# A two-layer decoder trunk on one core: the fourth token form laid with the others, and the first weight unit of each group laid apart

## The chip, the core and the metric

The kernel runs on one core of one Trainium2 chip. The metric is the device time of one execution in microseconds. The kernel before takes 1856.49 us, the median of three runs (1855.77 to 1856.5).

## What is computed

The reference is a decoder trunk of two layers over 512 tokens of width 1024, all in float32. Each layer is a feed-forward, a token mixer with memory heads beside it, and a second feed-forward, each followed by a layer norm of the scaled residual:

```python
x = layer_norm(DN_ALPHA * x + 0.5 * swiglu(x, ffn_w_gu[layer, 0], ffn_w_down[layer, 0]), ...)
o_tok, q_mem = mla_mix(...) if layer < N_A_LAYERS else nsa_mix(...)
o_mem = memory_attention(q_mem, mem, w_mem_kv[layer])
x = layer_norm(DN_ALPHA * x + jnp.concatenate([o_tok, o_mem], -1) @ w_out[layer], ...)
x = layer_norm(DN_ALPHA * x + 0.5 * swiglu(x, ffn_w_gu[layer, 1], ffn_w_down[layer, 1]), ...)
```

The first layer's mixer is latent attention, the second's a sparse attention of three branches. The four feed-forwards, `swiglu(x, w_gu, w_down) = (silu(x @ w_g) * (x @ w_u)) @ w_down` with an inner width of 2816, are most of the work, and the change is in them.

## The kernel before

**Split numbers.** TensorE multiplies float32 in a rounded form (`F32R`), so every operand is split in a high part and the rest: `split` (line 194) makes the high part by a cast on ScalarE (L199) and the low part by a subtraction on VectorE (L200). A product is three matmuls: high by high, high by low, low by high. Weights come in units of 128 partitions x 1024 floats, 512 KB each. `prep` (line 154) loads the next unit of a fixed order into `wraw` by a DMA from the SP queue, takes a pair of tiles `whi` and `wlo` for it, and splits it. The pair comes from `wring` (three pairs) or, inside the feed-forward scopes, from `W.extra` (four pairs more) in turn. `_unit_order` (line 53) writes that order out, and `unit(name, idx, look)` hands out the next pair after preparing units up to `look` further on.

**The feed-forward.** `ffn(l, f, ...)` (line 457) works on 22 column blocks (each 128 columns of w_g and the same 128 of w_u), which `GROUPS` cuts into five groups. A block of kind "s" is done plainly: two units, each multiplied with all of x by `feature_major` (L363, L365, L368: 48 matmuls of 256 columns a unit, 24 for each half of the tokens). A block of kind "d" is done by `seven` (line 482): the two 1024 x 128 matrices and the two halves of the tokens are a 2 x 2 product in blocks, and it is computed with seven products instead of eight, from sums and differences of the weights (`combined`, line 131, units g0 to g3) and of the tokens. One of the seven products is a `quarter` (line 370), 12 matmuls of 256 columns:

```python
for k in range(4):
    nc.tensor.matmul(ps, lhsT=hi[:, ks], rhs=xh[:, k], ...)   # L376
    nc.tensor.matmul(ps, lhsT=hi[:, ks], rhs=xl[:, k], ...)   # L377
for k in range(4):
    nc.tensor.matmul(ps, lhsT=lo[:, ks], rhs=xh[:, k], ...)   # L380
```

The order in a block is: unit g0 with the inputs themselves twice (`quarters(0, 0)`, `quarters(1, 0)`); unit g1 with form 4 and then form 1; unit g2 with forms 2 and 3; unit g3 with the inputs once (`quarters(1, 1)`). The four forms are sums and differences of the token blocks, made once for a feed-forward by `token_forms` (line 388) and kept split, each in two tiles `t1h`, `t1l` to `t4h`, `t4l` of the pool `F.fm`, called `t` in the profile. In the matmul the weights are the stationary operand and the tokens the moving one.

After the blocks of a group come its down projections (`by_units`, or `token_major` for the last group): there the activations `hhi`, `hlo` are stationary and the weight units `whi`, `wlo` move, 512 columns a matmul (L411 to L416, in the last group also L351 to L353). Then the next group begins with a g0 unit. In the first group of ffn(0,0), ffn(0,1) and ffn(1,1) (`halves` is true) three plain blocks come first: their six units are gone through for the first 256 tokens and then for the second 256. In ffn(1,0) two plain blocks come first, unit by unit.

**Where tiles lie.** A pool's tiles lie one behind the other in the order of their first use, pools on the left grow up from the bottom of SBUF, those opened by `right_pool` down from the top. Tiles called "place" or "offset" are never written: they fix the order, or shift what follows. `open_f` (line 262) lays out `F.fm` in that way, with a shift of 80 floats (320 bytes) ahead of form 4. A pool with `reuse_waits="tile"` makes a new tile wait for those older tiles that lay where it lies.

**What sets the order.** Within one engine's queue the framework issues by readiness and program order in its own model of time; only a few DMAs are pinned. TensorE's matmuls stand in the order that the program names.

Of the kernel before, what the change touches and what calls it, by code (L numbers as in the profile page):

```python
# [9 lines left out]
F32 = mybir.dt.float32  # L10
F32R = mybir.dt.float32r
# [6 lines left out]
P = 128  # L18
T = 512
# [32 lines left out]

def _unit_order():

    order = []

    def ffn(l, f, s):
        for m0, items in _groups(l, f):
            m = m0
            for it in items:  # L60
                if it == "d":
                    order.extend((f"g{i}", (l, f, m), 1024, s) for i in range(4))
                else:
                    order.extend(("gu", (l, f, m, g), 1024, s) for g in range(2))
                m += 1
            for i in range(m0, m):
                order.append(("dn", (l, f, i), 1024, s))

    ffn(0, 0, 0)
    for l in range(2):  # L70
        for i in range(4):
            order.append(("wm", (l, i), 1024, 0))
    for i in range(4):
        order.append(("wc", (i,), 832, 0))
    for i in range(2):
        order.append(("wqm", (i,), 1024, 0))
    order.append(("wuv", (), 768, None))
    order.append(("wuk", (), 768, None))
    for i in range(3):
        order.append(("wuq", (i,), 1024, None))  # L80
    for k in MIXORDER:
        order.append(("wo", (0, k), 1024, 1))
    ffn(0, 1, 1)
    for i in range(4):
        order.append(("wkf", (i,), 1024, 1))
    for i in range(2):
        order.append(("wvv", (i,), 1024, 1))
    for j in range(2):
        for i in range(4):
            order.append(("w1", (j, i), 1024, 1))  # L90
    for j in range(2):
        order.append(("w2", (j,), 256, 1))
    ffn(1, 0, 1)
    for i in range(3):
        order.append(("wgq", (i,), 876, 1))
    for i in range(6):
        order.append(("wq", (i,), 1024, 1))
    for k in MIXORDER:
        order.append(("wo", (1, k), 1024, 2))
    ffn(1, 1, 2)  # L100
    return order


@with_exitstack
def tile_trunk(ctx: ExitStack, tc, a: dict, out):
    nc = tc.nc
    order = _unit_order()

    const = ctx.enter_context(tc.tile_pool(name="const", bufs=1))
    wraw = ctx.enter_context(tc.tile_pool(name="wraw", bufs=NRAW))  # L110
# [7 lines left out]
    class W:  # L118
        pos = 0
        done = 0  # L120
        scope = None
        extra = None
        count = 0
        early = 0
        ready = {}
# [28 lines left out]
    def prep():  # L154
        name, idx, n, scope = order[W.done]
        if name in ("g0", "g1", "g2", "g3"):
            raw = combined(name, idx)
            n = 512 if name == "g3" else n
        else:
            src = a[name]  # L160
            for i in idx:
                src = src[i]
            raw = load(src, n)
        pool, tag = wring, "r"
        if scope is not None and W.scope is not None:
            W.count += 1
            if W.count % (NRING + NEXTRA) in EXTRA:
                pool, tag = W.extra, "x"
        hi = pool.tile([P, 1024], F32R, tag=tag + "h", name="whi")
        lo = pool.tile([P, 1024], F32R, tag=tag + "l", name="wlo")  # L170
        eng = nc.vector
        for c in ((slice(0, n),) if W.done else (slice(0, 512), slice(512, 1024))):
            split(hi[:, c], lo[:, c], raw[:, c], eng=eng)
        W.ready[W.done] = (hi, lo)
        W.done += 1
# [87 lines left out]
    def open_f(scope):  # L263
        F.st = ExitStack()
        W.extra = F.st.enter_context(tc.tile_pool(name=f"wx{scope}", bufs=NEXTRA, reuse_waits="tile"))
        F.xp = F.st.enter_context(tc.tile_pool(name=f"xp{scope}", bufs=1, reuse_waits="tile"))
        F.xp.tile([P, 112], F32, name="offset")
        F.sm = F.st.enter_context(tc.tile_pool(name=f"sm{scope}", bufs=2, reuse_waits="tile"))
        F.x = [F.xp.tile([P, D], F32, name=f"x{t}") for t in range(NT)]
        F.bk = 0  # L270
        W.scope = scope
        W.count = 0
        F.fst = ExitStack()
        F.fm = F.fst.enter_context(tc.tile_pool(name=f"fm{scope}", bufs=1, reuse_waits="tile"))
        for i in (1, 2, 3, 0, 4):
            for e in "hl":
                if i:
                    F.fm.tile([P, 4, 256], F32, tag=f"t{i}{e}", name="place")
            if not i:
                F.fm.tile([P, 80], F32, name="offset")  # L280

    def close_f():
        F.st.close()
# [4 lines left out]
    def right_pool(name, bufs=1):  # L288
        st = ExitStack()
        pool = st.enter_context(tc.tile_pool(name=name, bufs=bufs, side="right", reuse_waits="tile"))  # L290
        return st, pool
# [164 lines left out]

    def ffn(l, f, i, halves, spill=None, final=False, mid=None, hook=None):
        hst, hp = right_pool(f"h{l}{f}")
        if hook is None:
            load_gb(l, i)  # L460
        groups = _groups(l, f)
        for gi, (m0, items) in enumerate(groups):
            n = len(items)
            hhi = hp.tile([P, 5, T], F32R, tag="hhi", name="hhi")
            hlo = hp.tile([P, 5, T], F32R, tag="hlo", name="hlo")

            def fbank():
                F.bk += 1
# [1044 lines left out]
```

## Time and profile before

| | |
|---|---|
| median of 3 runs | 1856.49 us |
| the profiled execution | 1857.48 us |
| its span, first to last instruction | 1855.6 us |
| mean granted clock | 0.997 |
| TensorE busy | 1833.6 us (99%) |
| VectorE / ScalarE busy | 1463.0 us (79%) / 869.6 us (47%) |
| 256-column matmuls of `quarter`, L376, L377, L380 | 2156 on each line |

A matmul's duration in the profile includes the way through the array, so matmuls that follow one another overlap: what one costs in a stream is the distance from its start to the next start. In the timeline, matmuls of one kind that follow each other are drawn together (x4, x8). PEld is the loading of the stationary operand for the next matmul, which runs beside the present one.

### The profile page before, as it was taken

What the parts mean: (1) busy time and instruction counts of PE and PEld (TensorE: products, weight loads), DVE (VectorE), ACT (ScalarE), POOL (GpSimd) and SP (SyncE); (2) the same over time, 40 slices, a digit from 0 to 9 for tenths busy, and PEclk for the clock granted to TensorE, in tenths of its full rate; (3) what the DMA queues carried; (4) which work ended last, traced back from release to release, by engine and by line L of the source; (5) the groups of instructions that cost most, each with busy time, mean ns of one, the idle gap of its engine ahead of it and who ended that gap; (6) DMA issues with size and microseconds to landing.
All of it is one profiled execution on the core that took longest, in us unless ns stands there. A gap on an engine that the chain in (4) does not pass through costs nothing.

```text
span 1855.6 us, 31915 instructions
## 1 busy us (share of the span) xinstructions
PE 1833.6 (99%) x12776; PEld 1652.6 (89%) x12776; DVE 1463.0 (79%) x2362; ACT 869.6 (47%) x1435; POOL 162.6 (9%) x185
## 2 busy tenths in 40 slices
PE   9999999999999999999999999999999999999998
PEld 8899899896789899899999998998956789999997
DVE  7798788758668789788897987987567478887887
ACT  6344345456645345334653433444466444434432
POOL 0000000025500000000100000001255200000000
PEclk9999999999999999999999999999999999999999
DMA  6333334530234234234433323334321224323322
GB/s 241 114 114 103 125 103 146 177 114 24 69 114 145 75 102 134 80 103 148 130 120 113 126 84 110 114 121 158 110 46 29 113 75 131 114 80 114 118 81 75
DMA packets 59700, 203.85 MB, mean 110 GB/s; under 512 B 6944, under 2 KB 7216, under 8 KB 59552
## 3 DMA queue, kind: packets, MB, share of 16 engines
q1 hardware_dynamic: 56848, 194.18, 32.5%
q0 software_dynamic: 2416, 7.11, 1.2%
q8 instruction: 101, 1.65, 0.4%
q10 hardware_dynamic: 288, 0.52, 0.1%
q14 instruction: 47, 0.39, 0.1%
HBM read 188.16 MB, written 7.34 MB: 105 GB/s over the span
## 4 chain that ended last, share of the span: by engine, by line
PE 92%; DVE 4%; ACT 2%; issue 1%; POOL 1%; DMA 0%; POOLq 0%; DVEq 0%; ACTq 0%
PE bank L376 13%; PE bank L380 13%; PE bank L377 13%; PE bank L411 5%; PE bank L412 5%; PE bank L413 5%; PE bank L414 5%; PE bank L415 5%; PE bank L416 5%; PE bank L365 3%; PE bank L368 3%; PE bank L363 3%; PE tb L618 2%; PE o L646 2%; PE s L1190 1%; PE bank L352 1%
## 5 line engine op out<-in xcount | busy, mean ns | idle before, releaser
L199 ACT CAST whi<-wraw 128x1024 fp32r<-128x1024 f32 (+3 forms) x479 | 463.3, 976 | 548.0 <-PE bank L416 246.1
L200 DVE TENSOR_TENSOR wlo<-wraw,whi 128x1024 fp32r<-128x1024 f32 (+3 forms) x479 | 539.1, 1132 | 132.9 <-ACT whi L199 132.0
L376 PE MATMUL bank<-t,whi 128*128 128x256 f32 x1232 | 298.4, 278 | 0.0
L377 PE MATMUL bank<-t,whi 128*128 128x256 f32 x1232 | 297.9, 278 | 0.0
L377 PEld LDWEIGHTS bank<-t,whi 128*128 128x128 f32 x1232 | 231.9, 188 | 0.0
L376 PEld LDWEIGHTS bank<-t,whi 128*128 128x128 f32 x1232 | 231.8, 188 | 0.0
L377 PE MATMUL bank<-xlo,whi 128*128 128x256 f32 x924 | 222.0, 277 | 0.0
L376 PE MATMUL bank<-xhi,whi 128*128 128x256 f32 x924 | 222.0, 277 | 0.0
L380 PE MATMUL bank<-t,wlo 128*128 128x256 f32 x1232 | 191.8, 278 | 0.0
L377 PEld LDWEIGHTS bank<-xlo,whi 128*128 128x128 f32 x924 | 173.6, 188 | 0.6
L376 PEld LDWEIGHTS bank<-xhi,whi 128*128 128x128 f32 x924 | 173.6, 188 | 0.6
L380 PEld LDWEIGHTS bank<-t,wlo 128*128 128x128 f32 x1232 | 164.2, 189 | 0.0
L315 DVE SCALAR_TENSOR_TENSOR x<-x,bank 128x512 f32<-128x512 f32 x176 | 112.5, 682 | 56.9 <-PE bank L415 53.5
L380 PE MATMUL bank<-xhi,wlo 128*128 128x256 f32 x924 | 143.0, 277 | 0.0
L365 PE MATMUL bank<-xlo,whi 128*128 128x256 f32 x544 | 131.1, 281 | 1.2 <-DVE xlo L200 1.2
L363 PE MATMUL bank<-xhi,whi 128*128 128x256 f32 x544 | 131.3, 282 | 0.7 <-ACT xhi L199 0.7
L412 PE MATMUL bank<-whi,hhi 128*128 128x512 f32 x336 | 131.0, 390 | 0.0
L414 PE MATMUL bank<-wlo,hhi 128*128 128x512 f32 x336 | 130.9, 390 | 0.0
L411 PE MATMUL bank<-whi,hhi 128*128 128x512 f32 x336 | 130.8, 390 | 0.0
L415 PE MATMUL bank<-whi,hlo 128*128 128x512 f32 x336 | 130.8, 389 | 0.0
L413 PE MATMUL bank<-wlo,hhi 128*128 128x512 f32 x336 | 130.8, 389 | 0.0
L416 PE MATMUL bank<-whi,hlo 128*128 128x512 f32 x336 | 130.8, 389 | 0.0
(330 smaller groups left out, 3533.3 us busy)
## 6 DMA issues: line engine op xcount, KB each, us to landing
wraw<-in_gu SPq DMA_DIRECT2D x175, 512.0 KB, 3.3
wraw<-in_dn SPq DMA_DIRECT2D x88, 512.0 KB, 3.8
wraw<-in_wo SPq DMA_DIRECT2D x16, 512.0 KB, 3.5
wraw<-in_wm SPq DMA_DIRECT2D x8, 512.0 KB, 4.0
x_dram<-x SPq DMA_DIRECT2D x8, 512.0 KB, 3.0
x<-x_dram SPq DMA_DIRECT2D x8, 512.0 KB, 4.3
wraw<-in_w SPq DMA_DIRECT2D x8, 512.0 KB, 4.2
wraw<-in_wq SPq DMA_DIRECT2D x6, 512.0 KB, 3.4
```

The source lines that it names most:

```text
L199: nc.scalar.copy(hi, src)
L200: eng.tensor_tensor(lo, src, hi.bitcast(F32), op=ALU.subtract)
L363: nc.tensor.matmul(ps[:, c0:c1], lhsT=hi[:, k * P:(k + 1) * P], rhs=F.xhi[:, k, c0:c1], start=k == 0, stop=False)
L376: nc.tensor.matmul(ps, lhsT=hi[:, ks], rhs=xh[:, k], start=k == 0, stop=False)
L377: nc.tensor.matmul(ps, lhsT=hi[:, ks], rhs=xl[:, k], start=False, stop=False)
L380: nc.tensor.matmul(ps, lhsT=lo[:, ks], rhs=xh[:, k], start=False, stop=k == 3)
L411: nc.tensor.matmul(p0, lhsT=ahi, rhs=hi[:, 0:512], start=first, stop=False)
L412: nc.tensor.matmul(p1, lhsT=ahi, rhs=hi[:, 512:1024], start=first, stop=False)
L413: nc.tensor.matmul(p0, lhsT=ahi, rhs=lo[:, 0:512], start=False, stop=False)
L414: nc.tensor.matmul(p1, lhsT=ahi, rhs=lo[:, 512:1024], start=False, stop=False)
L415: nc.tensor.matmul(p0, lhsT=alo, rhs=hi[:, 0:512], start=False, stop=last)
L416: nc.tensor.matmul(p1, lhsT=alo, rhs=hi[:, 512:1024], start=False, stop=last)
```

## The change

Form 4 loses the shift ahead of it and lies right behind form 3. The pool of each feed-forward (`hp`) gets a fixed layout: `hhi`, `hlo`, three `sg` tiles, a shift of 48 floats, a new tile "apart" of 1024 floats, and 80 floats to fill up. The high part of the first weight unit of each group is put into that tile instead of the ring's; its low part stays in the ring. The very first group of all is left out; in ffn(1,0) the first group's unit is that of its first seven-product block. In the others' first groups it is the first plain unit.

```diff
 def _unit_order():
-    order = []
+    order, apart = [], set()
     def ffn(l, f, s):
         for m0, items in _groups(l, f):
             m = m0
+            if order:
+                apart.add(len(order) + (2 * items.index("d") if (l, f) == (1, 0) else 0))
...
-    return order
+    return order, apart
...
-        hi = pool.tile([P, 1024], F32R, tag=tag + "h", name="whi")
+        hi = (W.apart.tile([P, 1024], F32R, tag="apart", name="whi") if W.done in apart else
+              pool.tile([P, 1024], F32R, tag=tag + "h", name="whi"))
         lo = pool.tile([P, 1024], F32R, tag=tag + "l", name="wlo")
...
-        for i in (1, 2, 3, 0, 4):
+        for i in range(1, 5):
             for e in "hl":
-                if i:
-                    F.fm.tile([P, 4, 256], F32, tag=f"t{i}{e}", name="place")
-            if not i:
-                F.fm.tile([P, 80], F32, name="offset")
+                F.fm.tile([P, 4, 256], F32, tag=f"t{i}{e}", name="place")
...
     def ffn(l, f, i, halves, spill=None, final=False, mid=None, hook=None):
         hst, hp = right_pool(f"h{l}{f}")
+        for e in "hl":
+            hp.tile([P, 5, T], F32, tag="h" + e, name="place")
+        for e in range(3):
+            hp.tile([P, T], F32, tag="sg", name="place", bufs=3)
+        hp.tile([P, 48], F32, name="offset")
+        hp.tile([P, 1024], F32, tag="apart", name="place")
+        hp.tile([P, 80], F32, name="rest")
+        W.apart = hp
...
-            hhi = hp.tile([P, 5, T], F32R, tag="hhi", name="hhi")
-            hlo = hp.tile([P, 5, T], F32R, tag="hlo", name="hlo")
+            hhi = hp.tile([P, 5, T], F32R, tag="hh", name="hhi")
+            hlo = hp.tile([P, 5, T], F32R, tag="hl", name="hlo")
```

More of the change, by code (lines that the diff above doesn't have):

```diff
@@ L106, in tile_trunk @@
     nc = tc.nc
-    order = _unit_order()
+    order, apart = _unit_order()
     const = ctx.enter_context(tc.tile_pool(name="const", bufs=1))
@@ L122, in tile_trunk @@
         extra = None
+        apart = None
         count = 0
```

## The prediction

> **What bounds the kernel now.** I read the page first: engine shares, the granted clock, the chain that ended last.
>
> ```profile
> PE 1833.6 (99%) x12776; PEld 1652.6 (89%) x12776; DVE 1463.0 (79%) x2362; ACT 869.6 (47%) x1435; POOL 162.6 (9%) x185
> PEclk9999999999999999999999999999999999999999
> PE 92%; DVE 4%; ACT 2%; issue 1%; POOL 1%; DMA 0%; POOLq 0%; DVEq 0%; ACTq 0%
> ```
>
> TensorE is busy 99% of the span, at full granted clock, and it is 92% of the chain. Next came the view of what TensorE waits for; its two rows that touch the feed-forward matmuls are these.
>
> ```profile
> PE bank L365 <- DVE xlo L200: 1.2, 1, 1.2
> PE bank L363 <- ACT xhi L199: 0.7, 1, 0.7
> ```
>
> Both are single waits. No row names L376, L377 or L380, the lines of `quarter`, in which the matrices in the seven-product form are computed. So in the feed-forward parts only the distance between one matmul's start and the next counts, and that is read in the timeline. Here are the starts of the quarters (12 matmuls of 256 columns each) of the first two matrices of the third group of the first feed-forward. Columns: start, duration, engine, line, tiles.
>
> ```profile
> 149.60 0.28 PE L376 MATMUL bank<-xhi,whi 128*128 128x256 f32 x1
> ...
> 151.01 0.28 PE L376 MATMUL bank<-xhi,whi 128*128 128x256 f32 x1
> ...
> 152.42 0.28 PE L376 MATMUL bank<-t,whi 128*128 128x256 f32 x1
> ...
> 153.38 0.64 PE L380 MATMUL bank<-t,wlo 128*128 128x256 f32 x4
> 153.86 0.29 PE L376 MATMUL bank<-t,whi 128*128 128x256 f32 x1
> ...
> 154.33 0.28 PE L376 MATMUL bank<-t,whi 128*128 128x256 f32 x1
> ...
> 155.24 0.28 PE L376 MATMUL bank<-t,whi 128*128 128x256 f32 x1
> ...
> 156.60 0.28 PE L376 MATMUL bank<-t,whi 128*128 128x256 f32 x1
> ...
> 157.96 0.28 PE L376 MATMUL bank<-xhi,whi 128*128 128x256 f32 x1
> ...
> 159.32 0.28 PE L376 MATMUL bank<-xhi,whi 128*128 128x256 f32 x1
> ...
> 160.68 0.28 PE L376 MATMUL bank<-xhi,whi 128*128 128x256 f32 x1
> ...
> 162.04 0.28 PE L376 MATMUL bank<-t,whi 128*128 128x256 f32 x1
> ...
> 162.98 0.64 PE L380 MATMUL bank<-t,wlo 128*128 128x256 f32 x4
> 163.46 0.29 PE L376 MATMUL bank<-t,whi 128*128 128x256 f32 x1
> ...
> 163.93 0.28 PE L376 MATMUL bank<-t,whi 128*128 128x256 f32 x1
> ...
> 164.84 0.28 PE L376 MATMUL bank<-t,whi 128*128 128x256 f32 x1
> ```
>
> The same 12 matmuls take three times. The first two quarters take 1.41 us each (149.60 to 151.01 to 152.42). The third, the one with form 4, takes 1.44, and the one after it 1.38. From 155.24 on every quarter takes 1.36, and it stays so into the second matrix, until form 4 comes again at 162.04: 1.42, then 1.38, then 1.36. So there is a slow gait (1.41 a quarter, 118 ns a matmul) and a fast one (1.36, 113 ns), each of which lasts; and form 4 costs 0.08 us each time (0.06 in its quarter, 0.02 in the next) but leaves the stream in the fast gait, whichever it came in. A first matrix takes 159.32 - 149.60 = 9.72 us, a later one 2 x 1.36 + 1.42 + 1.38 + 3 x 1.36 = 9.60; without form 4's price it would be 7 x 1.36 = 9.52.
>
> What sets form 4 apart is its address. In the kernel's own allocation, taken modulo 512 bytes, all weights start at 256, the inputs xhi, xlo and forms 1 to 3 at 192, and form 4 at 0, because 320 bytes of padding lie ahead of it. A matmul runs while the next one's weights load, so what meets is moving data at 192 against weights at 256, but for form 4 data at 0 against weights at 256: 256 apart. That this distance is the cause is my inference; the row shows only that the quarter is slower and what follows is fast.
>
> The slow gait comes in with each group. First and last of the 16 later groups (four in each of four feed-forwards), whose first quarters take 1.41:
>
> ```profile
> 89.31 0.28 PE L376 MATMUL bank<-xhi,whi 128*128 128x256 f32 x1
> ...
> 90.72 0.28 PE L376 MATMUL bank<-xhi,whi 128*128 128x256 f32 x1
> ...
> 1787.01 0.28 PE L376 MATMUL bank<-xhi,whi 128*128 128x256 f32 x1
> ...
> 1788.42 0.28 PE L376 MATMUL bank<-xhi,whi 128*128 128x256 f32 x1
> ```
>
> First groups differ. The rows below are, in order: ffn(0,0), already fast ahead of its first form 4 (45.16 - 43.80 = 1.36); ffn(0,1), whose plain matrices run slow to the end (2.83 us for 24 matmuls, 583.77 to 586.60); ffn(1,0), slow as well (2.83); ffn(1,1), slow (2.82) until a break near 1520 and fast from there (2.72).
>
> ```profile
> 43.80 0.62 PE L380 MATMUL bank<-xhi,wlo 128*128 128x256 f32 x4
> 45.16 0.62 PE L380 MATMUL bank<-xhi,wlo 128*128 128x256 f32 x4
> ...
> 583.77 1.11 PE L368 MATMUL bank<-xhi,wlo 128*128 128x256 f32 x8
> 586.60 1.10 PE L368 MATMUL bank<-xhi,wlo 128*128 128x256 f32 x8
> ...
> 961.52 1.11 PE L368 MATMUL bank<-xhi,wlo 128*128 128x256 f32 x8
> 964.35 1.11 PE L368 MATMUL bank<-xhi,wlo 128*128 128x256 f32 x8
> ...
> 1515.47 1.11 PE L368 MATMUL bank<-xhi,wlo 128*128 128x256 f32 x8
> 1518.29 1.10 PE L368 MATMUL bank<-xhi,wlo 128*128 128x256 f32 x8
> 1522.01 1.07 PE L368 MATMUL bank<-xhi,wlo 128*128 128x256 f32 x8
> 1524.73 1.07 PE L368 MATMUL bank<-xhi,wlo 128*128 128x256 f32 x8
> ```
>
> **The change part by part.** No instruction is added or removed: the same casts, subtractions, DMAs and matmuls, at other addresses. Dropping the padding puts form 4 at 192 with the others. The new tile's place follows from its pool: the pool grows by 192 + 4096 + 320 = 4608 = 9 x 512 bytes, so its start stays at 256; ahead of the tile lie 20480 + 6144 bytes (52 x 512) and 192, so it starts at 448. That is 192 off the other weights, and 256 off the inputs at 192: form 4's distance, seen from the weights' side. I take the 448 from the sizes over the 256 of the words.
>
> *Form 4 back among the others.* It saves 0.08 us in each matrix in which another kick, or a fast gait already there, does its work. There are 17 seven-product matrices in a feed-forward's later groups and 2, 2, 3 and 2 in the first groups: 77.
>
> *The kick moved to the first unit.* The price has no row; the nearest is form 4. Only the high part lies apart, so 8 of a quarter's 12 matmuls meet the distance, and the last four play form 4's aftermath. Entered slow: 153.38 - 152.42 = 0.96 for the eight, and 154.33 - 153.86 = 0.47 for the four after: 1.43. Entered fast (the unit's second quarter): 162.98 - 162.04 = 0.94, and 163.93 - 163.46 = 0.47: 1.41. A first matrix then takes 1.43 + 1.41 + 5 x 1.36 = 9.64 instead of 9.72. At the low end the kick costs nothing (two quarters of 1.36): 0.12 less in each of 17 groups, 2.0 us, or 2.2 with the plain units. At the high end it costs as much as all of form 4's twelve (1.44 and 1.42 and 0.02 behind): 0.04 more, 0.7 in all. I take 9.64, since form 4's row is the same distance.
>
> *Sum.* Later groups: 16 first matrices and 52 others, 0.08 each: 5.44. First groups: ffn(0,0) and (1,1), two matrices each, fast already: 4 x 0.08 = 0.32; ffn(0,1), kicked in its plain matrices: (9.72 - 9.52) + 0.08 = 0.28; ffn(1,0), whose new tile is its first seven-product unit: 3 x 0.08 = 0.24. Plain matrices of ffn(0,1): 12 half units at 2.83; the kicked unit's two stay there (0.96 + 0.96 + 0.47 + 0.45 = 2.84), ten fall to 2.72: 1.10. A break by transposes inside them may bring the slow gait back until the kicked unit's second half, 2.6 half units at 0.11; half of that is 0.14. Plain matrices of ffn(1,1): 2.4 half units gain 0.26, the kicked unit's second half loses 0.10, the break 0.14: nothing. In all 5.44 + 0.84 + 0.96 = 7.24 us. The profiled execution took 1857.48 (span 1855.6), so 1850.24 for it; it was 0.99 above the median of the runs, 1856.49, so 1849.3.
>
> *Costed at nothing.* The faster stream must still be fed. VectorE is the tight one, by the table of stretches:
>
> ```profile
> 149.00:197.00 48.00, 48.00 (x418) 47.88 (x417) 46.55 (x75) 25.11 (x33) 0.00 (x0) 1.00 0.47 154
> 62.00:89.00 27.00, 27.00 (x122) 22.38 (x121) 15.50 (x23) 5.97 (x7) 0.00 (x0) 1.00 0.18 57
> ```
>
> It is busy 46.55 of 48.00 us in the seven-product stretch, but only 15.50 of 27.00 in a down projection, where it catches up by splitting units ahead; 0.4 us less in a stretch is small beside that 11.5. The clock column is 1.00, so the gaits aren't the clock. If that cover were gone, TensorE would wait and the 7 us would stay unearned.
>
> *A rule against it.* The Trainium skill, "TensorE: Matmul & The Clock Gate", step-by-step section, says that TensorE reads moving data and weights through two independent ports, so that loading the next weights takes nothing from the running matmul. By that rule addresses are no matter and the time stays 1856.5; the 1.36, 1.41 and 1.44 of equal quarters at one clock disagree.
>
> **The rivals.** *A. The weights' address does not kick* (what matters is the moving data's own place, or the true distance is another). Then nothing ends the slow gait: every quarter after a down projection takes 1.41, a matrix 7 x 1.41 = 9.87. Sum: 16 x 0.15 + 52 x 0.27 = 16.4, ffn(0,1) 0.42, ffn(1,0) 0.69, less 0.32: 17.2 slower, 1873.7. For it: no row has weights at another place. Against: loading and streaming are symmetric in a distance.
>
> *B. The kick's second quarter leaves the stream slow.* It is entered fast and lasts 8, not 12; in all rows form 4 has 12. Each later group runs 1.43 + 1.41 + 5 x 1.41 = 9.89 and then 9.87: 16 x 0.17 + 52 x 0.27 = 16.8, ffn(1,0) 0.71, less 1.6 from the other first groups: 15.9, so 1872.4. It decides early: a matrix that stays slow costs 0.35 against my forecast, so 21 of the 77, five groups, eat the gain.
>
> *C. The new tile waits for older memory.* In ffn(0,1) and (1,1) it lies where the mixed heads of the output projection lay.
>
> ```profile
> 549.22 3.90 ACT L199 CAST whi<-wraw 128x1024 fp32r<-128x1024 f32 x4 [0.91 <-PE bank L353]
> 551.78 1.09 PE L339 MATMUL bank<-cst,x 128*128 128x128 f32 x8
> ```
>
> The first casts start at 549.22. If the tile must wait for the projection's last matmul, at about 551.9, ScalarE stands 2.7 us, behind it the other casts and the last tile's norm; twice 2.7 is 5.4, and 1854.7 results. Against: by the order of the tags the tile lies on mx7 and mx0, which are read early.
>
> *D. The address is no matter,* and gait and form 4 have another cause: no change, 1856.5. Against it stand 77 form 4's that all cost the same.
>
> **How the numbers follow.** The forecast 0.76, A 0.06, B 0.06, C 0.06, D 0.03; 0.03 for a reordered issue of either sign. About 0.2% (3.7 us) is what a measurement tells from no change. Faster is the forecast and part of the rest: 0.78; within 0.2% C and D: 0.09; slower A and B and a rest: 0.13. The likeliest alone spans 1847.1 (kick free) to 1850.0. The range goes on to C and D, and a little below for a gait that ends earlier: 1846.5 to 1857.5; above it lies 0.13.
>
> **What would show it.** In the timeline after: form 4's quarter at 1.36 in every matrix; the first unit's two quarters at about 1.43 and 1.41; from the third quarter 1.36; later matrices 9.52. The plain matrices of ffn(0,1) at 2.72 but for the first unit. Wrong would be quarters of 1.41 past the first unit (A if from the start without a change, B if after two), or a wait at L363 or L376 (C).

## The result and the profile after

The changed kernel takes 1880.73 us (median of 4 runs, 1879.63 to 1883.02), the kernel before on the same chip 1856.13 (4 runs, 1854.04 to 1856.5). The ratio is 1.0134, 95% interval 1.0122 to 1.0147: 24.6 us slower, where 7.2 us faster was predicted. The profiled execution took 1879.63 with a span of 1877.9, against 1855.6 before. In the changed kernel `quarter` has its matmuls on L379, L380 and L383 (L376, L377 and L380 before), and `feature_major` on L366, L368 and L371.

The page of the changed kernel: TensorE's row, the granted clock, the chain that ended last.

```profile
PE 1854.0 (99%) x12776; PEld 1672.4 (89%) x12776; DVE 1467.0 (78%) x2362; ACT 865.3 (46%) x1435; POOL 166.7 (9%) x185
PEclk9999999999999999999999999999999999999999
PE 89%; DVE 5%; issue 2%; ACT 2%; POOL 1%; DMA 1%; POOLq 0%; DVEq 0%; ACTq 0%
```

The same 12776 matmuls, the same clock; TensorE's busy time alone grew by 20.4 us (1833.6 to 1854.0). So it is the stream itself that is slower. Here are the quarters of the third group of the first feed-forward, as in the prediction; the columns are start, duration, engine, line, tiles.

```profile
150.92 0.28 PE L379 MATMUL bank<-xhi,whi 128*128 128x256 f32 x1
...
152.34 0.28 PE L379 MATMUL bank<-xhi,whi 128*128 128x256 f32 x1
...
153.76 0.28 PE L379 MATMUL bank<-t,whi 128*128 128x256 f32 x1
...
155.18 0.28 PE L379 MATMUL bank<-t,whi 128*128 128x256 f32 x1
...
159.42 0.28 PE L379 MATMUL bank<-xhi,whi 128*128 128x256 f32 x1
...
163.66 0.28 PE L379 MATMUL bank<-t,whi 128*128 128x256 f32 x1
```

The first unit's two quarters take 1.42 us each (150.92 to 152.34 to 153.76), about what the prediction gave them. Form 4, the next quarter, now costs no more than its neighbours. But nothing becomes fast: 153.76 to 159.42 is 5.66 for four quarters, 1.41 each, and 159.42 to 163.66 is 4.24 for three. In the kernel before, the stream went at 1.36 from the fifth quarter of this group on. The same holds in all 16 later groups. Over the 539 quarters of the program the starts add up to 741.3 us before and 762.1 after (the 505 outside the first units run at 117.8 ns a matmul, 1.41 a quarter): 20.8 of the 22.3 us between the two spans.

The unit laid apart even ends a fast gait that is already there. In ffn(1,0) the plain matrices happened to run fast in this execution; then the unit comes. A row below holds the last eight matmuls of half a plain unit (L371) or the last four of a quarter (L383), so that from row to row of L383 is one quarter's worth.

```profile
972.44 1.07 PE L371 MATMUL bank<-xhi,wlo 128*128 128x256 f32 x8
975.16 1.07 PE L371 MATMUL bank<-xhi,wlo 128*128 128x256 f32 x8
977.02 0.64 PE L383 MATMUL bank<-xhi,wlo 128*128 128x256 f32 x4
978.45 0.63 PE L383 MATMUL bank<-xhi,wlo 128*128 128x256 f32 x4
979.86 0.63 PE L383 MATMUL bank<-t,wlo 128*128 128x256 f32 x4
981.28 0.64 PE L383 MATMUL bank<-t,wlo 128*128 128x256 f32 x4
```

Before the unit a half unit takes 2.72 (fast), after it a quarter takes 1.41 to 1.42 (slow), to the end of the group.

### The profile page after: what moved, and what is told of

It is laid out like the page before. It is cut to its first block, busy times and chain, and to the rows that moved or that the text cites. A ratio compares the mean times of both kernels' runs of the same rounds, so it can differ in the third digit from the quotient of the medians.

```text
span 1877.9 us, 31839 instructions
## 1 busy us (share of the span) xinstructions
PE 1854.0 (99%) x12776; PEld 1672.4 (89%) x12776; DVE 1467.0 (78%) x2362; ACT 865.3 (46%) x1435; POOL 166.7 (9%) x185
## 4 chain that ended last, share of the span: by engine, by line
PE 89%; DVE 5%; issue 2%; ACT 2%; POOL 1%; DMA 1%; POOLq 0%; DVEq 0%; ACTq 0%
PE bank L379 14%; PE bank L380 14%; PE bank L383 14%; PE bank L418 4%; PE bank L417 4%; PE bank L414 4%; PE bank L415 4%; PE bank L416 4%; PE bank L419 4%; PE bank L371 3%; PE bank L368 3%; PE bank L366 3%; PE tb L629 2%; PE o L657 2%; PE s L1201 1%
## 5 line engine op out<-in xcount | busy, mean ns | idle before, releaser
L379 PE MATMUL bank<-t,whi 128*128 128x256 f32 x1232 | 304.2, 281 | 0.0
L380 PE MATMUL bank<-t,whi 128*128 128x256 f32 x1232 | 304.2, 281 | 0.0
L380 PEld LDWEIGHTS bank<-t,whi 128*128 128x128 f32 x1232 | 232.7, 189 | 0.0
L379 PEld LDWEIGHTS bank<-t,whi 128*128 128x128 f32 x1232 | 232.6, 189 | 0.0
L380 PE MATMUL bank<-xlo,whi 128*128 128x256 f32 x924 | 228.5, 281 | 0.0
L379 PE MATMUL bank<-xhi,whi 128*128 128x256 f32 x924 | 228.5, 281 | 0.0
L383 PE MATMUL bank<-t,wlo 128*128 128x256 f32 x1232 | 195.4, 281 | 0.0
L380 PEld LDWEIGHTS bank<-xlo,whi 128*128 128x128 f32 x924 | 174.8, 189 | 0.6
L379 PEld LDWEIGHTS bank<-xhi,whi 128*128 128x128 f32 x924 | 174.7, 189 | 0.6
L383 PEld LDWEIGHTS bank<-t,wlo 128*128 128x128 f32 x1232 | 167.9, 190 | 0.0
L331 POOL TENSOR_TENSOR st<-st,cst 128x1 f32<-128x1 f32 x24 | 21.3, 889 | 1497.8 <-DVE st L330 1497.7
L383 PE MATMUL bank<-xhi,wlo 128*128 128x256 f32 x924 | 146.5, 281 | 0.0
L368 PE MATMUL bank<-xlo,whi 128*128 128x256 f32 x544 | 131.3, 281 | 1.0 <-DVE xlo L206 1.0
L366 PE MATMUL bank<-xhi,whi 128*128 128x256 f32 x544 | 131.5, 282 | 0.4 <-ACT xhi L205 0.4
L418 PE MATMUL bank<-whi,hlo 128*128 128x512 f32 x336 | 130.8, 389 | 0.0
```

The lines of the kernel that those rows point to most:

```text
L366: nc.tensor.matmul(ps[:, c0:c1], lhsT=hi[:, k * P:(k + 1) * P], rhs=F.xhi[:, k, c0:c1], start=k == 0, stop=False)
L368: nc.tensor.matmul(ps[:, c0:c1], lhsT=hi[:, k * P:(k + 1) * P], rhs=F.xlo[:, k, c0:c1], start=False, stop=False)
L379: nc.tensor.matmul(ps, lhsT=hi[:, ks], rhs=xh[:, k], start=k == 0, stop=False)
L380: nc.tensor.matmul(ps, lhsT=hi[:, ks], rhs=xl[:, k], start=False, stop=False)
L383: nc.tensor.matmul(ps, lhsT=lo[:, ks], rhs=xh[:, k], start=False, stop=k == 3)
L418: nc.tensor.matmul(p0, lhsT=alo, rhs=hi[:, 0:512], start=False, stop=last)
```

## The experiments

"Place" is an address modulo 256 or 512 bytes, as said; "distance" is the moving data's place minus the weights', modulo 256. Ordinary is 192 - 256, so 192. Places are worked out from the sizes of the tiles and the starts that the prediction gives. A "kick" is a stretch of matmuls for which one side has stepped to another place. Form 4 in the kernel before (0 against 256) and the changed kernel's unit (192 against 448) both have a distance of 0. Where a median of several runs is given it has its interval; the others are single executions, beside which the kernel before took 1855.82 to 1856.91 (one execution, or the median of 9 or 19). Executions of one kernel differ by up to 6 us (1849.8 to 1856.14 in experiment 6), so the single ones are read by their quarters more than by their times. Diffs are against the changed kernel.

**1 and 2. One part alone.** The first keeps the unit apart and lays form 4 back at 0; the second lays form 4 with the others and no unit apart.

```diff
 # e1_form4_back: open_f as in the kernel before
-        for i in range(1, 5):
+        for i in (1, 2, 3, 0, 4):
...
 # e2_no_apart
-            if order:
+            if False:
```

> The changed kernel with form 4 back behind its 320 bytes of padding (0 modulo 512); the first unit's high part stays apart. Theory M (only a jump in the address of the moving data sets the stream fast; weights elsewhere don't): every form 4 sets it fast again, later quarters 1.36 us, form 4's 1.42, and the first unit's two at 1.42 and 1.43 as in the changed kernel; the time is that of before plus about 17 x 0.03 and a little in the plain units, 1857 to 1858. Theory S (the weight tile apart is what makes the stream slow): the slow gait stays somewhere, the time lies well above 1860.

> The changed kernel with form 4 among the others and no weight unit put apart (the pool keeps its layout). M: nothing sets the stream fast, quarters stay at 1.41 in all later groups, the first unit's too; first groups may be fast by chance; 1874 to 1881. S: without the tile apart the stream is fast in each group, quarters of 1.36 from the start, about 1848.

Measured: 1859.77 with form 4 back, 1873.89 without either. The third group with form 4 back (L386 there stands for L383):

```profile
151.87 0.63 PE L386 MATMUL bank<-xhi,wlo 128*128 128x256 f32 x4
153.29 0.64 PE L386 MATMUL bank<-t,wlo 128*128 128x256 f32 x4
154.70 0.62 PE L386 MATMUL bank<-t,wlo 128*128 128x256 f32 x4
156.06 0.62 PE L386 MATMUL bank<-t,wlo 128*128 128x256 f32 x4
```

Form 4's quarter ends with the row of 153.29; the row of 156.06 comes 1.36 after that of 154.70: the fast gait is there at once. So form 4 was the thing that made the groups fast, and the unit apart doesn't do its work. The time is 3.6 us over the kernel before, where 1857 to 1858 was expected. Only 0.5 us of it is in the quarters (741.8 against 741.3); 2.9 us is in the plain matrices of ffn(0,1) and ffn(1,1), which experiment 9 takes up. Without either, all 28 or 35 quarters of each of the 16 later groups take 1.41. The loss against the kernel before, 17.7 us, is close to what the prediction worked out for its rival A (17.2), in which nothing ends the slow gait.

**3. Longer at that place.** In two feed-forwards the first unit's low part lies apart too (at 448), so that all 24 matmuls of the unit have the distance 0, as all of form 4's have.

```diff
-        lo = pool.tile([P, 1024], F32R, tag=tag + "l", name="wlo")
+        lo = (W.apart.tile([P, 1024], F32R, tag="apartl", name="wlo")
+              if W.done in apart and W.scope != 1 else
+              pool.tile([P, 1024], F32R, tag=tag + "l", name="wlo"))
```

> The changed kernel with the low part of the first unit apart too, 448 modulo 512, in ffn(0,0) and ffn(1,1) alone: 12 of a quarter's 12 matmuls meet the distance of 256, as with form 4 before. Theory L (eight were too few): the later groups of these two feed-forwards go on at 1.36 after the first unit, 34 matrices at 9.52 instead of 9.89, 12 to 13 us less than the changed kernel, about 1868. M: they stay at 1.41, about 1881.

Measured: 1879.29. In the groups concerned the first two quarters take 1.43 to 1.44, and then the stream is as slow as with the high part alone. That the kick was too short, or was broken off by the low part, is out.

**4. Other places for the tile**, one in each feed-forward: 0, 192, 384 and 128 modulo 512.

```diff
-        hp.tile([P, 48], F32, name="offset")
+        o = {(0, 0): 64, (0, 1): 112, (1, 0): 32, (1, 1): 96}[l, f]
+        hp.tile([P, o], F32, name="offset")
...
-        hp.tile([P, 80], F32, name="rest")
+        hp.tile([P, 128 - o], F32, name="rest")
```

> The changed kernel with the tile apart at another place in each feed-forward: 0 modulo 512 in ffn(0,0) (256 off the other weights), 192 in ffn(0,1) (as the moving data), 384 in ffn(1,0), 128 in ffn(1,1). Theory D (the weights' side can do it, at another distance): in at least one feed-forward the later groups go on at 1.36, some 6 us less each, 1874 or below. M: all later groups at 1.41, 1878 to 1883.

Measured: 1864.0. The third groups of the second (192) and of the last feed-forward (128):

```profile
701.11 0.64 PE L383 MATMUL bank<-xhi,wlo 128*128 128x256 f32 x4
702.53 0.63 PE L383 MATMUL bank<-xhi,wlo 128*128 128x256 f32 x4
703.95 0.64 PE L383 MATMUL bank<-t,wlo 128*128 128x256 f32 x4
705.36 0.63 PE L383 MATMUL bank<-t,wlo 128*128 128x256 f32 x4
...
1660.24 0.63 PE L383 MATMUL bank<-xhi,wlo 128*128 128x256 f32 x4
1661.62 0.62 PE L383 MATMUL bank<-xhi,wlo 128*128 128x256 f32 x4
1662.98 0.62 PE L383 MATMUL bank<-t,wlo 128*128 128x256 f32 x4
```

At 192 it is as at 448: 1.42, 1.42, then 1.41. At 128 only the unit's first quarter is slow, and from its second on a quarter takes 1.36 (the 1.38 between the first two rows still holds the last four matmuls of the slow quarter). 384 behaves as 128. At 0 nothing happens: 1.41 throughout, as without a unit apart; modulo 256 it is the place of the other weights, so the distance is the ordinary one. So a weight unit can end the slow gait, but not from the changed kernel's place; and places that differ by 256 behave alike.

**5 and 6. The tile at 128, and at 384, in all feed-forwards.** The edit is that of experiment 4 with one shift, 96 or 32 floats, for 48.

> The changed kernel with the tile apart at 128 modulo 512 in all four feed-forwards instead of 448. Theory P (what counts is the step of the weights' place when the stream goes back from the tile apart to the ring, taken modulo 256: a step of 128 sets it fast, a step of 64 back from 448 or 192 sets it slow): in each later group the first quarter takes 1.41 and all others 1.36, as in ffn(1,1) with other places; matrices at 9.52 to 9.57 instead of 9.60 and 9.72; 1846 to 1850, faster than both kernels. Theory Q (the fast gait there came from that feed-forward's own state): only some groups are fast, 1855 to 1875.

> The same with the tile apart at 384 modulo 512. P: 384 and 128 are the same place modulo 256, so the same gaits and a time within 2 us of the tile at 128, 1846 to 1850. If the place counts modulo 512: a time or gaits of its own. Q: 1855 to 1875.

Measured: 1853.64 at 128 (ratio 0.9983, 0.9975 to 0.9992) and 1852.84 at 384 (0.998, 0.9969 to 0.9991). In both, each later group has one quarter of 1.41 and then only 1.36. The quarters add up to 733.9 us, 7.4 less than before, but the time fell by only 2.9 and 3.7 (in 5 and 6). So theory P had the gaits right and the time, 1846 to 1850, wrong. Where the rest went is the question of experiment 9.

**7. Other places for form 4**, with no unit apart: 256 modulo 512 in the first feed-forward, 320 in the second and third, 384 in the last.

```diff
+                F.fm.tile([P, (16, 32, 48)[scope]], F32, name="offset")   # ahead of form 4
```

> No tile apart; form 4 at 256 modulo 512 in ffn(0,0), at 320 in the scope of ffn(0,1) and ffn(1,0), at 384 in ffn(1,1) (before: 0 everywhere). Period of 256: ffn(0,0) is as before, form 4's quarter 1.42, 1.44 where it comes in slow, 1.38 behind it and then 1.36. Period of 512: ffn(0,0) shows something else. For 320 and 384 no row exists: by P, in its form for the moving data, steps of 128 and more may set the stream fast without a price, quarters at 1.36 or 1.41 in place of 1.42; if only 0 modulo 256 does it, the later groups there stay at 1.41.

Measured: 1866.69. The rows of 699.36 and 1664.28 end form 4's quarter in the third groups of the second and last feed-forward (L386 for L383):

```profile
697.94 0.64 PE L386 MATMUL bank<-xhi,wlo 128*128 128x256 f32 x4
699.36 0.63 PE L386 MATMUL bank<-t,wlo 128*128 128x256 f32 x4
700.77 0.63 PE L386 MATMUL bank<-t,wlo 128*128 128x256 f32 x4
...
1664.28 0.65 PE L386 MATMUL bank<-t,wlo 128*128 128x256 f32 x4
1665.69 0.62 PE L386 MATMUL bank<-t,wlo 128*128 128x256 f32 x4
1667.05 0.62 PE L386 MATMUL bank<-t,wlo 128*128 128x256 f32 x4
```

256 acts as 0 did in the kernel before. 384 (distance 128) also makes the stream fast (1.36 from 1665.69 to 1667.05). 320 (distance 64) does not: 1.41 goes on. Nor does it end a fast gait: the first group of ffn(1,0) came in at 1.36, its form 4 took 1.41, and 1.36 went on behind it. So the two sides don't answer each other. Distance 64 makes the stream fast when the weights step there (experiments 5 and 6) and not when the data do; distance 0 makes it fast when the data step there and slow when the weights do.

**8. Finer places for the tile**: 64, 96, 160 and 32 modulo 512 in the four feed-forwards (edit as in experiment 4).

> The changed kernel with the tile apart at 64 modulo 512 in ffn(0,0), 96 in ffn(0,1), 160 in ffn(1,0) and 32 in ffn(1,1). P: 96 and 160, near 128, set the later groups fast (quarters of 1.36 from the second or third on); 32 and 64 are open: slow (1.41) if they behave like 0, fast if the border lies below them. Each feed-forward whose later groups are fast is some 6 us less than the changed kernel's.

Measured: 1851.56. All four places leave the stream at 1.36 after two quarters of 1.38 to 1.43. Of the places tried for the weights, only 192 modulo 256, the changed kernel's, leaves it slow.

**9 and 10. The unit at the entry.** In ffn(0,1) and ffn(1,1) the unit apart was the first plain one, met right behind the output projection. Both runs lay the first seven-product unit apart instead; the ninth with the tile at 128, the tenth at the changed kernel's 448.

```diff
-                apart.add(len(order) + (2 * items.index("d") if (l, f) == (1, 0) else 0))
+                apart.add(len(order) + 2 * items.index("d"))
```

> The tile apart at 128 modulo 512, as in the run that had it there in all groups, but in the first groups of the second and the last feed-forward it holds the first unit of the first seven-product block, not the first plain unit (as ffn(1,0) has it already). In that earlier run the work between the output projection and the plain matrices stood in another order than in the kernel before and took about 2 us longer at each of the two places (from 513.9 us to the first seven-product matrix 74.15 us against 73.36, although its matrices were in the fast gait and should have saved 1.2). If the order comes from the tile at that place (theory E), the stretches return to 73.4 us or less and the time is about 1849.5 to 1851. If the order has another cause (theory N), it stays at about 1853.6. Quarters: only the first of each later group at 1.41 us, the rest 1.36; the plain matrices of the two feed-forwards slow or fast by chance, the seven-product ones fast from the second quarter of the apart unit.

> The changed kernel (tile at 448 modulo 512), with the same one edit: in the first groups of the second and the last feed-forward the unit laid apart is the first seven-product one. Theory E: about 4 us less than the changed kernel's 1880.7, so 1876 to 1878, and the order at the two entries again that of the kernel before, which prices the share of the change's loss that isn't the gait. Theory N: 1880. In both, nearly all quarters after the apart unit stay at 1.41 us.

Measured: 1848.28 (5 runs, 1847.98 to 1851.46; before 1855.82; ratio 0.9963, 0.9949 to 0.9977) and 1876.11 (1.0107, 1.0093 to 1.0121); the first is a little under the 1849.5 to 1851 expected. Compared with experiment 5 and with the changed kernel that is 5.4 and 4.6 us less; both differences are between kernels run at different times. The entry of ffn(0,1) with the plain unit apart (experiment 5):

```profile
549.08 2.00 ACT L205 CAST whi<-wraw 128x1024 fp32r<-128x1024 f32 x2 [0.45 <-PE bank L356]
551.60 0.28 PE L366 MATMUL bank<-xhi,whi 128*128 128x256 f32 x1
...
553.27 1.09 PE L342 MATMUL bank<-cst,x 128*128 128x128 f32 x8 [0.45 <-DVE x L337]
553.97 1.08 ACT L205 CAST xhi<-bank 128x512 fp32r<-128x512 f32 x2 [2.88 <-PE bank L342]
554.12 0.37 PE L366 MATMUL bank<-xhi,whi 128*128 128x256 f32 x1
```

And with the seven-product unit apart (experiment 9):

```profile
547.13 3.90 ACT L205 CAST whi<-wraw 128x1024 fp32r<-128x1024 f32 x4 [0.90 <-PE bank L356]
549.70 1.09 PE L342 MATMUL bank<-cst,x 128*128 128x128 f32 x8
550.55 0.36 PE L366 MATMUL bank<-xhi,whi 128*128 128x256 f32 x1
```

In the first, ScalarE casts two weight tiles instead of four, TensorE runs some matmuls of a plain unit ahead of the last tile's transposes (L342), and those then wait for VectorE. In the second the order is that of the kernel before. The view of waits, over the whole span, in experiment 5:

```profile
PE bank L342 <- DVE x L337: 6.5, 14, 0.6
```

and in experiment 9:

```profile
PE bank L342 <- DVE x L337: 3.6, 8, 0.5
```

The kernel before has 3.6 in 8 waits too, the changed kernel 5.9 in 14. From the profile of 5 to that of 9 the plain matrices of the two feed-forwards shrink by 1.1 us each, and the matmuls of all projections by 1.3 together: 3.5 us, which I put down to the two entries. Why the issue order changes with the tile isn't shown.

Experiments 9 and 10 differ in one thing, the address of 19 weight tiles, and by 27.8 us. The sums over the quarters differ by 27.6 (733.9 against 761.5).

**11 and 12. Nothing steps.** No unit apart, form 4 with the others, but the ordinary distance is another: 128, 64 and 0 in experiment 11, 160, 96 and 224 in experiment 12 (first feed-forward; second and third; last).

```diff
-        F.xp.tile([P, 112], F32, name="offset")
+        F.xp.tile([P, (96, 80, 128)[scope]], F32, name="offset")     # e11
+        F.xp.tile([P, (104, 88, 120)[scope]], F32, name="offset")    # e12
```

> No unit apart and form 4 with the others, so that no address changes inside a feed-forward; but the inputs and all four forms lie at another ordinary place: 128 (modulo 256) in the first feed-forward, 64 in the second and third, 0 in the last, instead of 192; weights stay at 256. That is moving data minus weights, modulo 256, of 128, 64 and 0. Theory G (the two gaits are a thing of any steady distance, and what the down projection leaves is always the slow one): all later groups at 1.41 us a quarter, about 1874, as without any unit apart at the old place. Theory H (each distance has its own gait): 128 and 64, which set the fast gait when the apart tile brought them, run at 1.36 us or settle there by themselves; 0, which left the slow gait, runs at 1.43 or more. Then the first three feed-forwards gain and the last one loses: about 1855 to 1860.

> As the run with other ordinary distances (no unit apart, form 4 with the others, no address changed inside a feed-forward), but inputs and forms at 160 modulo 256 in the first feed-forward, at 96 in the second and third, at 224 in the last, weights at 256. So far steady distances (moving data minus weights, modulo 256) gave: 192 both gaits (1.36 and 1.41 us a quarter), 64 only 1.41, 128 and 0 only 1.43 to 1.44. Theory T (only a distance of 192 has a fast gait): no quarter under 1.41 in any of the three, the time 1875 to 1886. Theory U (distances in between the multiples of 64 have both gaits or the fast one, as the apart tile at 32, 96 and 160 modulo 512 also set the fast one): some of the three run at 1.36 with no address changed inside the feed-forward; one such feed-forward saves 6 to 7 us against a slow one.

Measured: 1885.72 and 1890.69. Third groups at the distances 128, 64 and 0 (experiment 11):

```profile
153.09 0.65 PE L383 MATMUL bank<-xhi,wlo 128*128 128x256 f32 x4
154.53 0.65 PE L383 MATMUL bank<-xhi,wlo 128*128 128x256 f32 x4
...
705.62 0.63 PE L383 MATMUL bank<-xhi,wlo 128*128 128x256 f32 x4
707.04 0.63 PE L383 MATMUL bank<-xhi,wlo 128*128 128x256 f32 x4
...
1674.78 0.64 PE L383 MATMUL bank<-xhi,wlo 128*128 128x256 f32 x4
1676.22 0.64 PE L383 MATMUL bank<-xhi,wlo 128*128 128x256 f32 x4
```

Every steady distance has its gait in the later groups: 1.44, 1.41 (705.62 to 707.04 is 1.42 in the rounded rows, 117.8 ns a matmul over the later groups) and 1.44 here; 1.42 at 160, 1.44 at 96 and 1.42 at 224. At 128 there is a second one, a little below: the first group of the first feed-forward, ahead of any down projection, ran at 118.6 ns a matmul, the later ones at 120.0. None of the six is ever fast. Where nothing steps, only 192 has a gait of 1.36, and a slow one beside it. The expectation that 64 and 128, which set the fast gait, would themselves be fast was wrong, and so were both theories' times in experiment 11 (1874; 1855 to 1860) and theory T's upper end in experiment 12 (1886): five of the six distances are slower than the slow gait at 192.

The prices of the quarters that step fit this where the data step: 1.41 at distance 64, 1.42 to 1.44 at distance 0. Where the weights step they don't always. In the first group of ffn(1,0) in experiment 5 the stream comes in fast, and eight matmuls at distance 64 stand between these two rows:

```profile
962.43 0.28 PE L379 MATMUL bank<-xhi,whi 128*128 128x256 f32 x1
...
963.34 0.62 PE L383 MATMUL bank<-xhi,wlo 128*128 128x256 f32 x4
```

They take 0.91 us, as eight of the fast gait do (8 x 0.113): nothing is paid. Form 4 at the same distance, in the same group of experiment 7, paid 1.41 for its quarter. So the side that steps counts for the price too, and the distance alone doesn't fix the pace.

**13. Twelve matmuls or twenty-four.** No unit apart; forms 4 and 1 at distance 0 in the first feed-forward (two quarters of one unit, 24 matmuls), forms 2 and 3 in the second and third, form 1 alone in the last.

```diff
-        for i in range(1, 5):
+        for i in ((2, 3, 0, 4, 1), (1, 4, 0, 2, 3), (2, 3, 4, 0, 1))[scope]:
...
+                F.fm.tile([P, 80], F32, name="offset")    # at the 0 of that list
```

> No weight unit apart. Instead of form 4 alone, forms 4 and 1 lie at 0 modulo 512 in the first feed-forward (two quarters after one another, 24 matmuls, the same unit), forms 2 and 3 in the second and third (24 matmuls too), form 1 alone in the last (12 matmuls, but the second quarter of its unit). The question is why distance 0 leaves the fast gait when the moving data step there for 12 matmuls and the slow one when the weights step there for 16 or 24. If the number of matmuls decides, the pairs leave the slow gait like the tile apart (all matrices of three feed-forwards at 1.41 us a quarter, 1870 or more in all) and form 1 alone leaves the fast one. If the side that steps decides, all of them leave the fast gait and cost only their own quarters, 1.42 to 1.44 us each: a second such quarter in each of 56 matrices, 0.07 each, 4 us, so about 1860.

Measured: 1861.14. The third group of the first feed-forward, from its second quarter on:

```profile
152.05 0.63 PE L386 MATMUL bank<-xhi,wlo 128*128 128x256 f32 x4
153.47 0.64 PE L386 MATMUL bank<-t,wlo 128*128 128x256 f32 x4
154.91 0.64 PE L386 MATMUL bank<-t,wlo 128*128 128x256 f32 x4
156.32 0.62 PE L386 MATMUL bank<-t,wlo 128*128 128x256 f32 x4
157.68 0.62 PE L386 MATMUL bank<-t,wlo 128*128 128x256 f32 x4
```

24 matmuls at distance 0, and the stream is fast behind them (156.32 to 157.68 is 1.36). All the arrangements leave it fast. So the number of matmuls doesn't decide: the side that steps does.

**14. Everything 64 bytes higher.** The changed kernel with inputs, forms and ring shifted together, the distance still 192; the tile at 192 modulo 256 in the first feed-forward (now distance 64), at 128 in the second (128), at 0 in the last two (0).

```diff
     const = ctx.enter_context(tc.tile_pool(name="const", bufs=1))
+    const.tile([P, 16], F32, name="offset")
...
-        hp.tile([P, 48], F32, name="offset")
+        o = {(0, 0): 48, (0, 1): 32, (1, 0): 64, (1, 1): 64}[l, f]
+        hp.tile([P, o], F32, name="offset")
```

> As the changed kernel, but inputs, forms and the weights' ring all lie 64 bytes higher (moving data at 0 modulo 256, weights at 64), so their distance stays 192 while all places change. The tile apart lies at 192 modulo 256 in the first feed-forward (the place that left the slow gait, now at a distance of 64 from the moving data), at 128 in the second (distance 128), and at 0 in the third and fourth (distance 0). If the distance decides, the first two run fast after the unit (64 and 128 did) and the last two slow: about 1864. If the place itself decides, the first one stays slow, the second runs fast (128 did), and the last two stay as the down projection leaves them, slow: about 1869; their first quarters tell the two apart as well, 1.43 us at distance 0 against 1.41.

Measured: 1874.94. The third groups of the first and third feed-forwards (L384 for L383):

```profile
153.54 0.62 PE L384 MATMUL bank<-xhi,wlo 128*128 128x256 f32 x4
154.90 0.62 PE L384 MATMUL bank<-xhi,wlo 128*128 128x256 f32 x4
...
1087.01 0.64 PE L384 MATMUL bank<-xhi,wlo 128*128 128x256 f32 x4
1088.44 0.64 PE L384 MATMUL bank<-xhi,wlo 128*128 128x256 f32 x4
1089.85 0.63 PE L384 MATMUL bank<-t,wlo 128*128 128x256 f32 x4
```

The place that left the slow gait before (192) now leaves the fast one, and 0, which did nothing, now leaves the slow one at 1.43 for the kicked quarter. The second feed-forward is fast. So it is the distance and not the place. The quarters add up to 749.1 us, halfway between the changed kernel's 762.1 and the 733.9 of experiment 5, as two feed-forwards of each kind should. The time alone would have misled: it is 11 us over the expected 1864 and nearer to the other theory's 1869. The matmuls of the projections, whose weights were shifted and whose activations were not, take 542.7 us instead of 536.7, and the plain matrices 3.5 us more than before; neither was in the expectation.

## Why the prediction was wrong

**The step that failed** is "The kick moved to the first unit", in its last sentence: "since form 4's row is the same distance". The sentence carries two things. The price was right: 1.43 and 1.41 were predicted for the unit's quarters and 1.42 and 1.42 to 1.43 came. (For the second there is luck in it: its 1.41 was for a quarter that comes in fast.) What the kick leaves behind was wrong. A distance of 0 reached by a step of the moving data leaves the stream fast (experiments 7 and 13), the same distance reached by a step of the weights leaves it slow (3, 10, and 14, where the place is another). In the prediction, "loading and streaming are symmetric in a distance" stood as the argument against rival A. It was the assumption itself, and no row bore on it, because "no row has weights at another place", which I had put on the other side.

**The inference about the distance** was half right. It is the distance modulo 256 (experiment 14; 128 and 384 alike in 5 and 6, 0 and 256 in 7), but not "256 apart" as one special meeting: of the weights' steps tried at an ordinary distance of 192, those to 32, 64, 96, 128 and 160 all set the fast gait.

**Form 4 back among the others** did what it should: its quarter costs nothing more, as the steady quarters of experiments 2 and 9 show. In experiment 9, where another unit does its work, the quarters add up to 7.4 us less than before; the prediction had 5.44 + 0.84 = 6.28 for them. The whole fell by 7.5 (1855.82 to 1848.28), against the 7.24 of the sum and a predicted time of 1849.3. That the totals lie so close is in part luck. The kick at 128 is cheaper than the one in the sum (a first matrix takes 9.57, not 9.64: 1.1 us in the 16 later groups), and experiment 9 kicks no plain matrix, where the sum had 0.96 to gain. It also differs from the changed kernel in two things, the tile's place and the unit at the two entries; with the place alone changed (experiment 5) the time fell by 2.9. So the 0.08 for each form 4 was right, but the whole sum needed both the fast gait and entries that lose nothing.

**The plain matrices of ffn(0,1)** were to gain 1.10; they lost 0.9 in the profiled execution, in which the entry had its other order and the unit apart ended a fast gait at the second half. Which gait plain matrices run in isn't settled by the addresses alone: those of ffn(0,0), where no unit lies apart, take 2.83 us a half unit in the changed kernel and 2.72 in experiment 10.

**Rival A** (1873.7) named the outcome, with nearly the right price for it (experiment 2: 1873.89) but not the reason, since the address does kick. **Rival B** (1872.4) described the groups as they run, slow after two kicked quarters, and gave length as the reason; experiments 3 and 13 rule that out. Both stood at 0.06, though the point that separates them from the forecast had no row at all. The 7 us by which the result lies above A can be sized from the sums, as an estimate: some 3.5 for the two entries, 1.6 in the seven-product matrices of the first groups (those of ffn(0,0) and ffn(1,1), fast in A, ran slow in this execution), and 2.0 in the later groups, where A left out the kicked quarters' price and counted 1.41 for 1.414.

**Rival C** had the right place and not the mechanism as priced: no 2.7 us of ScalarE standing ahead of the first casts, but a changed order of issue, in which ScalarE stands 2.88 us behind the first two casts (the row of 553.97 in experiment 5) until the transposes are done; some 3.5 us for the two entries, where it had 5.4. That older memory holds it up wasn't tried.

**Rival D,** the rule that addresses are no matter, is out: experiments 9 and 10 run the same instructions and differ by 27.8 us. The Trainium skill, "TensorE: Matmul & The Clock Gate", step-by-step section, has two independent read ports, so that loading weights takes nothing from the running matmul. By that rule, as the prediction read it, the two would take the same time; the runs disagree.

**Costed at nothing:** the feeding of the faster stream. It held. In experiment 9 nearly every quarter runs at 1.36 and the waits of TensorE are those of before.

## What to carry to other kernels

A cause read from one side of a symmetry (the moving operand) isn't evidence for the other side (the stationary one): where the whole sum hangs on such a transfer, give its failure the chance of an untested claim, and price the case in which the kick does harm. Where a stream has two lasting gaits, ask of each event two questions, what it costs and which gait it leaves, and try several places before choosing one: here 128 against 448 modulo 512 is 27.8 us out of 1850. And try a new tile at a unit that isn't met at a seam between stages: the same tile at the entry of a feed-forward went with another order of issue, some 1.8 us each time.

## What the runs showed of the hardware

With a weight load for each matmul of 256 columns, the time from start to start depends on the distance modulo 256 bytes between moving and stationary operand, and on what came before. Steady means over the later groups of a feed-forward in which nothing steps (experiments 2, 11 and 12), in ns a matmul at a mean granted clock of 0.997 to 0.999: 117.8 at 64, 118.3 at 224, 118.7 at 160, 120.0 at 0, 96 and 128 (118.6 in one first group at 128); at 192 117.8, or 113.3 in the fast gait, and whichever it is lasts for tens of us. Which of the two it is depends on the last step: down projections left it at 117.8 in all 16 later groups of experiment 2; a step of the weights to the distances 32, 64, 96, 128 or 160 or of the data to 0 or 128 leaves 113.3; a step of the weights to 0 leaves 117.8, also out of the fast gait; a step of the data to 64 leaves it as it was. The side also sets the price: in a fast stream, eight matmuls at distance 64 took the fast gait's 0.91 us where the weights had stepped (experiment 5), while the twelve of form 4 took 1.41 us, 118 ns each, where the data had (experiment 7). Why the side matters stays open: the runs separate the side from the number of matmuls and from the place, but none shows what happens between the two reads.

The fastest kernel seen is that of experiment 9, 1848.28 us, with the tile at 128 modulo 512 and never at a plain unit: ratio to the kernel before 0.9963 (0.9949 to 0.9977).
